# Waiting for the last stores in a section of their own: a grouped convolution on one core

## The chip, the cores and the metric

One core of a Trainium2 chip. The metric is the device time of one execution in microseconds. The program is built once and executed several times, and a difference below 2% counts as "same". An execution has two lengths: the timed number, and the span, which runs from the first to the last instruction recorded by the profile and is 1.8 to 1.9 us shorter in most executions of the kernel before.

## The reference

A 3x3 convolution with padding 1 in 8 groups: 16 images, 64 channels in, 128 out, 64 x 64 pixels, all float32. Cut to its core:

```python
for g in range(groups):
    for b in range(batch):
        for co in range(c_out_per_group):
            for ci in range(c_in_per_group):
                for kh in range(k):
                    for kw in range(k):
                        output[b, g * c_out_per_group + co] += \
                            weight[g * c_out_per_group + co, ci, kh, kw] * \
                            x_pad[b, g * c_in_per_group + ci, kh:kh+h, kw:kw+w]
```

The output is 33.55 MB and the input 16.8 MB.

## The kernel before

GpSimd loads bf16 pieces of the images, VectorE makes two shifted copies of each, TensorE multiplies into eight PSUM banks, ScalarE copies them out to one of five buffers `ob`, and the sync engine stores each buffer with one 2 MB transfer (the first image in two of 1 MB). A store has landed when it has raised its semaphore, a counter that an engine can wait for, by 16 (the trace of before has 272 landings for the 17 stores). The kernel places all waits itself, inside one section that the scheduler leaves alone (`tile_critical`). Cut to the part concerned:

```python
    with tc.tile_critical():
        program(nc, x, weight, out, U, ob, w_sb, wb, mask4, mask, ident, wt, banks)

def program(...):
    ...
    stored = [nc.alloc_semaphore(f"st{i}") for i in range(NOB)]      # NOB = 5
    uses = [0] * NOB
    for b in range(B):                                               # B = 16 images
        slot = b % NOB
        ...                                                          # matmuls, copies to ob[slot]
            if c1 > c0:
                SP.wait(wrote)
                nc.sync.dma_start(outf[b, :, c0:c1], ob[slot][:, c0:c1]).then_inc(stored[slot], 16)
                uses[slot] += 1
        ...
    POOL.wait(SP.done(nc.sync.nop()))
    nc.clear_and_free_semaphores(sems)          # two range clears on GpSimd

    for k in range(B, B + NOB):
        s, val = stored[k % NOB], 16 * uses[k % NOB]
        ...   # the sync engine waits for s >= val, then subtracts val
```

Behind a section the scheduler puts closing code of its own. The sync engine, which holds the section's last work, signals that it is over. All five engines drain (here: each runs one short instruction, with a record of 7 to 46 ns, which waits for that signal and reports that the engine has come so far). The sync engine collects the drains, and then come two barriers, at which every engine waits for all others, with a clear of semaphores between them (in the trace of before GpSimd sees the first one full at 123.124 us, starts the clear at 123.370 and sees the second one full at 123.544). The argument is about this code.

## Time and profile before

| | kernel before |
|---|---|
| timed, median of 3 | 125.62 us (125.61 to 125.66) |
| span of the profiled execution | 123.728 us |
| last instruction of a compute engine ends | 102.84 us |
| last of the five waits starts | 122.603 us |
| from there to the end of the span ("the tail") | 1.125 us |

### The profile page before, as it was taken

What the parts mean: (1) busy time and instruction counts of PE and PEld (TensorE: products, weight loads), DVE (VectorE), ACT (ScalarE), POOL (GpSimd) and SP (SyncE); (2) the same over time, 40 slices, a digit from 0 to 9 for tenths busy, and PEclk for the clock granted to TensorE, in tenths of its full rate; (3) what the DMA queues carried; (4) which work ended last, traced back from release to release, by engine and by line L of the source; (5) the groups of instructions that cost most, each with busy time, mean ns of one, the idle gap of its engine ahead of it and who ended that gap; (6) DMA issues with size and microseconds to landing.
All of it is one profiled execution on the core that took longest, in us unless ns stands there. A gap on an engine that the chain in (4) does not pass through costs nothing.

```text
span 123.7 us, 1308 instructions
## 1 busy us (share of the span) xinstructions
PE 93.3 (75%) x791; PEld 19.1 (15%) x197; DVE 82.3 (66%) x87; ACT 69.4 (56%) x72; POOL 27.8 (22%) x41
## 2 busy tenths in 40 slices
PE   5868999999669999999999999589999970000000
PEld 0011222222112222222222222011111100000000
DVE  3089999999999999999999999999900000000000
ACT  4099867676713776778767493579686782000000
POOL 5997040412230256272450000000000000000000
PEclk9999999999967999999999999999999997555555
DMA  3999999999999999999999999999999999999991
GB/s 75 270 210 217 212 212 297 297 297 331 336 344 339 339 429 363 334 344 350 347 342 339 315 342 368 421 429 424 429 424 434 429 440 445 434 424 424 429 424 69
DMA packets 4374, 42.46 MB, mean 343 GB/s; under 512 B 976, under 2 KB 976, under 8 KB 1360
## 3 DMA queue, kind: packets, MB, share of 16 engines
q1 hardware_dynamic: 2736, 34.38, 66.2%
q0 software_dynamic: 1632, 8.00, 31.5%
q8 instruction: 4, 0.07, 0.2%
q14 instruction: 2, 0.02, 0.0%
HBM read 16.81 MB, written 33.55 MB: 407 GB/s over the span
## 4 chain that ended last, share of the span: by engine, by line
PE 30%; DMA 24%; DVE 20%; ACT 5%; issue 4%; POOLq 0%; SPq 0%
PE banks L256 30%; DMA out_dram<-ob 20%; DVE U L198 20%; ACT ob L272 5%; DMA U<-in_x_dram 4%; DVE wt L214 0%; POOLq L336 0%; SPq L55 0%
## 5 line engine op out<-in xcount | busy, mean ns | idle before, releaser
L256 PE MATMUL banks<-U,wt 96*64 96x504 bf16 (+1 forms) x768 | 87.0, 385 | 5.1 <-DVE U L198 3.2
L198 DVE COPY U<-U 32x4096 bf16<-32x4096 bf16 (+2 forms) x80 | 80.3, 1004 | 5.5 <-DMA U<-in_x_dram 3.0
L272 ACT COPY ob<-banks 128x1024 f32<-128x1024 f32 x64 | 61.4, 1018 | 28.4 <-PE banks L256 19.2
L114 POOL DMA_DIRECT2D U<-in_x_dram x34 | 27.0, 802 | 36.9 <-PE banks L256 35.9
L246 PEld LDWEIGHTS <-wt 96*64 96x64 bf16 x192 | 18.7, 112 | 74.1 <-issue 65.6
L174 PE MATMUL banks<-ob 128*128 128x512 bf16 x20 | 6.1, 469 | 1.5 <-DVE mask L129 1.5
L205 ACT CAST U<-ob 32x1536 bf16<-32x1536 f32 x4 | 5.9, 1469 | 0.1
L165 ACT CAST wb<-w_sb 128x96 bf16<-128x96 f32 x3 | 0.9, 355 | 3.9 <-DMA w_sb<-in_weight_dram 3.9
L165 ACT ACT_TABLE_LOAD x1 | 1.3, 1283 | 1.0 <-SPq L55 1.0
L186 PE MATMUL banks<-ident,wb 128*96 128x128 bf16 x3 | 0.4, 232 | 1.4 <-ACT wb L165 1.4
L186 PEld LDWEIGHTS banks<-ident,wb 128*96 128x96 bf16 x3 | 0.2, 122 | 5.5 <-ACT wb L165 5.5
L128 DVE MEMSET ob<- 128x256 f32 x1 | 0.3, 272 | 1.1 <-SPq L55 1.1
L159 DVE TENSOR_REDUCE mask<-mask 128x4 f32<-128x16 f32 x1 | 0.2, 180 | 0.8 <-POOL mask L147 0.8
L214 DVE TENSOR_TENSOR wt<-banks,mask 96x384 bf16<-96x384 f32 x1 | 0.6, 554 | 0.0
L132 DVE MEMSET U<- 32x448 uint32 x1 | 0.4, 432 | 0.1
L131 DVE MEMSET U<- 32x448 uint32 x1 | 0.4, 432 | 0.0
L172 PEld LDWEIGHTS <-ob 128*128 128x128 bf16 x2 | 0.2, 102 | 1.5 <-DVE mask L129 1.5
L142 POOL TENSOR_SCALAR_AFFINE_SELECT ident<-ident 128x128 bf16<-128x128 bf16 x1 | 0.3, 300 | 0.0
L137 POOL TENSOR_SCALAR_AFFINE_SELECT mask<-mask 128x16 f32<-128x16 f32 x1 | 0.2, 228 | 0.1
L147 POOL TENSOR_SCALAR_AFFINE_SELECT mask<-mask 128x16 f32<-128x16 f32 x1 | 0.2, 214 | 0.0
L322 POOL MEMSET const-float32-0.0<- 128x1 f32 x1 | 0.1, 99 | 0.3 <-issue 0.3
L130 DVE MEMSET ident<- 128x64 uint32 x1 | 0.1, 112 | 0.0
(4 smaller groups left out, 0.4 us busy)
## 6 DMA issues: line engine op xcount, KB each, us to landing
out_dram<-ob SPq DMA_DIRECT2D x15, 2048.0 KB, 20.6
U<-in_x_dram POOLq DMA_DIRECT2D x26, 256.0 KB, 10.3
out_dram<-ob SPq DMA_DIRECT2D x2, 1024.0 KB, 12.7
ob<-in_x_dram SPq DMA_DIRECT2D x1, 768.0 KB, 4.8
U<-in_x_dram POOLq DMA_DIRECT2D x4, 160.0 KB, 5.3
U<-in_x_dram POOLq DMA_DIRECT2D x2, 132.0 KB, 5.0
U<-in_x_dram POOLq DMA_DIRECT2D x2, 124.0 KB, 4.5
w_sb<-in_weight_dram SPq DMA_DIRECT2D x1, 36.0 KB, 4.7
```

Of the source, the lines that this page charges most:

```text
L114: nc.gpsimd.dma_start(place(n, n % 3, h0, h1), xr[32 * n : 32 * n + 32, h0 * W : h1 * W]).then_inc(s, 16)
L131: DVE.done(nc.vector.memset(U[0:32, :, 1, :], 0.0))
L132: zeros = DVE.done(nc.vector.memset(U[64:96, :, H, :], 0.0))
L165: e = ACT.done(nc.scalar.copy(wb[:, kw, :].rearrange("p (j g c) -> p j g c", j=3, g=4), wv[:, kw].unsqueeze(2).to_broadcast([128, 3, 4, CIg]),
L174: nc.tensor.add_instruction(mybir.InstMatmult(name=nc.get_next_instruction_name(), engine=mybir.EngineType.PE, start_tensor_calc=True, sto ...
L186: ins = nc.tensor.matmul(banks[0:96, 0, 128 * kw : 128 * kw + 128], wb[:, kw, :], ident, start=True, stop=True,)
L198: c = DVE.done(nc.vector.tensor_copy(place(n, j, h0, h1), place(n, n % 3, h0, h1)))
L205: need = ACT.done(nc.scalar.copy(place(n, n % 3, 0, RROWS), raw[p0 : p0 + 32, 0 : RROWS * W]))
L214: w_need = DVE.done(nc.vector.tensor_mul(wt[0:96].rearrange("p t (h g c) -> p (t h) g c", h=2, g=4), banks[0:96, 0, 0 : 3 * 128].rearrange ...
L246: pe.ldweights(w_ap, **pos)
L256: ins = pe.add_instruction(mybir.InstMatmult(name=nc.get_next_instruction_name(), engine=mybir.EngineType.PE, start_tensor_calc=kw == 1, s ...
L272: wrote = free[pair] = ACT.done(nc.scalar.copy(ob[slot][:, o0 : o0 + 1024], banks[:, 2 * pair : 2 * pair + 2, :].rearrange("p k n -> p (k ...
```

## The change

Intent: the five waits need the sync engine alone. If they stand in a second section, the first one can be closed while the last stores are still on their way, so the other four engines' drains and the sync engine's waits for them lie under the stores.

```diff
     with tc.tile_critical():
-        program(nc, x, weight, out, U, ob, w_sb, wb, mask4, mask, ident, wt, banks)
+        rest = program(nc, x, weight, out, U, ob, w_sb, wb, mask4, mask, ident, wt, banks)
+
+    with tc.tile_critical():
+        for s, val in rest:
+            count_back(nc, s, val)
+
+def count_back(nc, s, val):
+    num = dict(sync_type="semaphore", id=s.num, ant_name=s.name)
+    nc.sync.add_instruction(mybir.InstEventSemaphore(...))   # wait s >= val, subtract val: as before
@@ end of program()
-    for k in range(B, B + NOB):
-        ...                                                   # the same five instructions
+    return [(stored[k % NOB], 16 * uses[k % NOB]) for k in range(B, B + NOB)]
```

More of the change, by code (lines that the diff above doesn't have):

```diff
@@ L55 @@
     with tc.tile_critical():
-        program(nc, x, weight, out, U, ob, w_sb, wb, mask4, mask, ident, wt, banks)
+        rest = program(nc, x, weight, out, U, ob, w_sb, wb, mask4, mask, ident, wt, banks)
[4 more added lines that the diff above has]
+    num = dict(sync_type="semaphore", id=s.num, ant_name=s.name)
+    nc.sync.add_instruction(mybir.InstEventSemaphore(
+        name=nc.get_next_instruction_name(), engine=mybir.EngineType.SP,
+        sync_info=mybir.SyncInfo(
+            on_wait=[mybir.SyncWait(wait_mode="sem-ge-imm", wait_value=val, **num)],
+            on_update=[mybir.SyncUpdate(update_mode="sem-sub-imm", update_value=val, **num)],
+        ),
+    ))
 class Order:
@@ L294, in program @@
     nc.clear_and_free_semaphores(sems)
-    for k in range(B, B + NOB):
-        s, val = stored[k % NOB], 16 * uses[k % NOB]
-        num = dict(sync_type="semaphore", id=s.num, ant_name=s.name)
-        nc.sync.add_instruction(mybir.InstEventSemaphore(
-            name=nc.get_next_instruction_name(), engine=mybir.EngineType.SP,
-            sync_info=mybir.SyncInfo(
-                on_wait=[mybir.SyncWait(wait_mode="sem-ge-imm", wait_value=val, **num)],
-                on_update=[mybir.SyncUpdate(update_mode="sem-sub-imm", update_value=val, **num)],
-            ),
-        ))
+    return [(stored[k % NOB], 16 * uses[k % NOB]) for k in range(B, B + NOB)]
 _INS = ['x', 'weight', 'groups']
```

## The prediction

> **What bounds the kernel now.** The change can only act after the last store has been issued, so I read the profile from its end: first the slices of the page, then what the sync engine's queue waited for, then a table of stretches of the tail, then the lines of the closing code, and last the starts of single records in the trace.
>
> The page's slices, for the matmuls, VectorE, ScalarE and the DMA engines (each slice is 123.7/40 = 3.1 us):
>
> ```profile
> PE   5868999999669999999999999589999970000000
> ...
> DVE  3089999999999999999999999999900000000000
> ACT  4099867676713776778767493579686782000000
> ...
> DMA  3999999999999999999999999999999999999991
> ```
>
> The compute engines are empty for the last seven slices, some 21 us, while the DMA engines are full up to the last slice. So the end is set by the stores still queued when computing stops. The page's chain of work that ended last stops at the last ScalarE copy (102.84 us), because it follows working instructions; its "DMA out_dram 20%" is an earlier wait for a free buffer, and the last 21 us are not in it. The waits of the sync engine's own queue show them:
>
> ```profile
> engine line waited for: us in total, times, longest us
> SPq L284 <- ACT ob L272: 95.4, 17, 13.1
> SPq L299 <- SPq L299: 19.3, 4, 4.9
> ```
>
> L299 are the five waits that the change moves. They are put down to each other, but what really ended each is a landing of a store. The stretches from the last issue to the end, cut at the five waits:
>
> ```profile
> core 0: us, PE busy (x) PEld busy (x) DVE busy (x) ACT busy (x) POOL busy (x), PEclk, DMA share, GB/s
> 103.00:108.00 5.00, 0.00 (x0) 0.00 (x0) 0.00 (x0) 0.00 (x0) 0.00 (x0) 0.55 0.99 423
> 108.00:112.90 4.90, 0.00 (x0) 0.00 (x0) 0.00 (x0) 0.00 (x0) 0.00 (x0) 0.50 1.00 428
> 112.90:117.70 4.80, 0.00 (x0) 0.00 (x0) 0.00 (x0) 0.00 (x0) 0.00 (x0) 0.50 1.02 437
> 117.70:122.60 4.90, 0.00 (x0) 0.00 (x0) 0.00 (x0) 0.00 (x0) 0.00 (x0) 0.50 0.72 308
> 122.60:123.75 1.15, 0.00 (x0) 0.00 (x0) 0.00 (x0) 0.00 (x0) 0.00 (x0) 0.50 0.00 0
> ```
>
> Four 2 MB stores leave at 423 to 437 GB/s with the DMA share at 1.0: nothing that an engine does in these stretches can make them shorter. Only the last row, 1.15 us without any transfer, is time of instructions. That is all that this change can touch. Two answers on the source lines say what stands there: the five waits, and the scheduler's own closing code on the line where the first section begins.
>
> ```profile
> L299 SPq EVENT_SEMAPHORE  x5: 17/17/17, 103.3 to 122.6; - x5
> ...
> L55 SPq EVENT_SEMAPHORE  x3: 17/28/28, 122.7 to 122.9; - x3
> ...
> L55 ACTq DRAIN  x1: 8/8/8, 122.7 to 122.7; - x1
> L55 POOLq DRAIN  x1: 46/46/46, 122.7 to 122.7; - x1
> ```
>
> The first of the five waits is satisfied at 103.3; the last begins at 122.6. Only after it, at 122.7, does every engine drain. Those five drains wait for nothing but the sync engine's signal, which it gives behind its five waits.
>
> The trace's single records give the tail in nanoseconds. The last data packet of the store queue ends at 122.198 and the last of the 16 landings is recorded at 122.586. The sync engine then starts, in turn: last wait 122.603; signal that the section is over 122.662; drain 122.734; a wait for VectorE's and TensorE's drains 122.808; a wait for its own and ScalarE's 122.882; a no-operation waiting for GpSimd's 122.954; a drain 123.028; a drain that reports to the first closing barrier 123.091. GpSimd sees that barrier full at 123.124; its range clear and a second barrier take until 123.728, the end of the span. In sum 122.603 to 123.091 is 0.488 us on the sync engine, then 0.033 to GpSimd, then 0.604: together 1.125 us.
>
> [...] a wait that held the queue for 4.8 us is a record of 17 ns, and records of 7 to 28 ns start 59 to 74 ns apart. So I cost a step by the distance between starts, never by its recorded length. [...] The trace has 0.39 us from last packet (122.198) to last landing (122.586)[...]. [...] at the start of this trace the sync engine's one is recorded at 33 ns and the next instruction starts 153 ns after its start. [...]
>
> **The change part by part.** No load, copy, matmul, ScalarE copy or store is moved: the comparison of the two built programs differs in line numbers, except on the sync engine, where some rows are new, and in branches at the end.
>
> Moved forward: the signal "section over", the five drains, and the sync engine's waits for the other four. They now come right behind the last issue. The sync engine signals at about 103.3; GpSimd is the last to answer, since its two semaphore clears end at 103.861. The drains then all end by about 104.0. These 0.15 to 0.2 us of the other engines were beside the sync engine's own chain anyway, and now lie under the stores.
>
> Added: an entry into the second section, in the built program one no-operation, three waits and one branch with a wait, all on the sync engine. At 74 ns a step, and 153 ns for the branch, 4 x 0.074 + 0.153 = 0.45 us, from 104.0 to about 104.5. The first wait comes due at 104.5 in place of 103.317, but its store has landed, and the second store lands only at 108.087. So 3.6 us of slack swallow it, and it costs nothing.
>
> Left behind the last wait: signal, drain, a no-operation waiting for that drain, a drain, the drain that reports to the barrier. Seven steps before become five. By the distances of before: 122.603 + 0.059 (signal) + 0.072 (drain) + 0.074 (no-operation) + 0.063 to 0.074 (drain; it waits for nothing now) + 0.063 (report) = 122.934 to 122.945, in place of 123.091. What goes is the two waits for the other engines' drains, 0.146 us, or 0.157 with the lighter drain. The 0.033 and 0.604 behind it stay: both barriers and the clear stand in the end block in both programs, and the other engines already wait there.
>
> Sum: 125.62 - 0.15 = **125.47 us**, 0.12% less. The 1.9 us between the timed 125.62 and the span of 123.7 I leave as they are.
>
> **The rivals.** First, that the whole closing time hides under the stores, which is what one may hope of such a change: 1.125 us off, 124.5 us, 0.9% less. For it: the other four engines are idle for 20 us. Against: the barriers and the final clear follow the second section in the built program, and need the sync engine, which cannot arrive before the last landing.
>
> Second, that nothing is gained: 125.62. For it: the sync engine itself needs the same signal and drain after the last landing, and the slowest other engine might have set the pace. Against: TensorE, the last of the others, reports to the barrier at 122.911, 0.18 us ahead of the sync engine's 123.091. So the sync engine's own chain sets it, and that chain loses two steps.
>
> Third, that it gets slower: the second section adds steps at its exit as well[...]. Exit steps that I take to be free (a branch that falls through) could cost 0.15 us as the measured one did, which just cancels the gain: 125.6. [...]
>
> Fourth, that the stores themselves land at another time. They run one behind the other from about 54 us with full DMA engines, and what comes before is not changed, so only chance moves them. The three runs of before lie within 0.05 us, but another build and another sitting can differ by more than that; I allow some 0.2 us.
>
> **Range and chances.** The step count gives 0.15 us with an uncertainty of one step either way, and chance between builds is larger than that. My range of 8 in 10 is 125.20 to 125.70, a little wider downward, since the first rival ends there in part. For 2%, 2.5 us would have to move. The only stretch the change touches is 1.125 us, so faster by over 2% is impossible by this reading (0.005); slower [...] (0.01); within 2% the rest (0.985).
>
> **What would show it.** In the profile after: the other four engines' drains near 103.3 to 104 instead of 122.7; the last of the five waits still at about 122.6; five sync records from it to the report instead of seven, and 0.97 to 0.98 us from it to the end of the span instead of 1.125. The stretches of the stores should read the same 423 to 437 GB/s. It is wrong if the last wait begins more than 0.2 us away from 122.6 (then the stores moved), if the tail stays at 1.12 us or grows (then the exit of the section costs what I take as free), or if the time falls by much more than 0.2 us (then something in the 1.9 us outside the span depends on the sections).

0.074 us a step and 0.153 us for the branch into the section are distances between starts in the trace of before, and the sum came to 125.62 - 0.15 = 125.47 us. The instruction recorded at 33 ns "at the start of this trace" is the sync engine's compare-and-branch, which also carries a wait.

## The result, and the profile after

Median 125.70 us in 4 runs (125.60 to 125.86) against 125.64 us in 4 runs of before: ratio 1.0001, 95% interval 0.9984 to 1.0019. A ratio is the mean time of one kernel's fast runs over that of the other's of the same rounds, so it is not quite the ratio of the medians quoted.

So the first comparison shows no gain. The profile shows one. The sync engine's own waits in the kernel after (engine and line, what it waited for, us in total, times, longest):

```profile
SPq L301 <- ACT ob L289: 95.5, 17, 12.7
SPq L67 <- SPq L67: 18.1, 4, 4.9
...
SPq L55 <- POOLq L55: 0.4, 1, 0.4
```

L67 are the same five waits. The last row is new: 0.4 us in which the sync engine waits for GpSimd's drain, after the last issue and long before the last landing. The records of the closing code of the two sections, L55 for the first and L59 for the second (duration min/median/max in ns, first and last start in us):

```profile
L67 SPq EVENT_SEMAPHORE  x5: 17/17/17, 104.6 to 122.8; - x5
...
L55 SPq EVENT_SEMAPHORE  x3: 17/28/28, 103.5 to 103.7; - x3
...
L55 ACTq DRAIN  x1: 8/8/8, 103.5 to 103.5; - x1
...
L55 POOLq DRAIN  x1: 46/46/46, 104.1 to 104.1; - x1
...
L59 SPq NOP  x2: 13/13/13, 104.2 to 123.0; - x2
L59 SPq EVENT_SEMAPHORE  x1: 17/17/17, 122.8 to 122.8; - x1
L59 SPq DRAIN  x1: 7/7/7, 122.9 to 122.9; - x1
```

The drains that stood at 122.7 now stand at 103.5 to 104.1, and behind the last wait are only a signal, a drain and a no-operation of the section, then the two drains that lead to the barrier. The stretches, cut at the five waits of this kernel (columns as in the prediction's table; the last two are the DMA share and GB/s):

```profile
103.00:108.00 5.00, 0.00 (x0) 0.00 (x0) 0.00 (x0) 0.00 (x0) 0.00 (x0) 0.65 1.00 429
108.00:113.00 5.00, 0.00 (x0) 0.00 (x0) 0.00 (x0) 0.00 (x0) 0.00 (x0) 0.50 0.99 426
113.00:117.90 4.90, 0.00 (x0) 0.00 (x0) 0.00 (x0) 0.00 (x0) 0.00 (x0) 0.50 1.01 435
117.90:122.75 4.85, 0.00 (x0) 0.00 (x0) 0.00 (x0) 0.00 (x0) 0.00 (x0) 0.50 0.69 297
122.75:123.75 1.00, 0.00 (x0) 0.00 (x0) 0.00 (x0) 0.00 (x0) 0.00 (x0) 0.50 0.00 0
```

The first three stretches have the same rate, 426 to 435 GB/s against 423 to 437 before. In both kernels the rate of the last of them falls before its end (308 and 297 GB/s over its stretch), and its sixteen parts land one after the other: from 121.171 to 122.586 us before, from 121.212 to 122.741 after. The last data packet of their queue ends at 122.198 and 122.405 us, 0.388 and 0.336 us ahead of the last landing. Step by step behind the last wait, starts in us from the traces' records:

| step | before | after |
|---|---|---|
| last of the five waits | 122.603 | 122.757 |
| signal that the section is over | 122.662 | 122.823 |
| the sync engine's own drain | 122.734 | 122.895 |
| wait for VectorE's and TensorE's drains | 122.808 | (at 103.626) |
| wait for its own and ScalarE's | 122.882 | (at 103.696) |
| no-operation (before: waits for GpSimd's drain; after: for its own) | 122.954 | 122.968 |
| drain | 123.028 | 123.012 |
| drain that reports to the first barrier | 123.091 | 123.076 |
| GpSimd sees the barrier full | 123.124 | 123.108 |
| end of the span | 123.728 | 123.712 |

From the last wait to the end: 123.728 - 122.603 = 1.125 us before, 123.712 - 122.757 = 0.955 us after. That is 0.170 us less. But the last store landed 0.154 us later in the profile of after, and nearly all of the gain is gone from the span. Two readings are open. In the first, the later landing is chance. In the second, the change causes it: another build, or closing work that disturbs the stores. If the second is right, the change gains nothing.

### The profile page after: what moved, and what is told of

Read it like the earlier page. It is cut to its first block, busy times and chain, and to the rows that moved or that the text cites. A ratio compares the mean times of both kernels' runs of the same rounds, so it can differ in the third digit from the quotient of the medians.

```text
span 123.7 us, 1316 instructions
## 1 busy us (share of the span) xinstructions
PE 94.1 (76%) x791; PEld 18.5 (15%) x197; DVE 82.2 (66%) x87; ACT 69.4 (56%) x72; POOL 27.7 (22%) x41
## 4 chain that ended last, share of the span: by engine, by line
PE 30%; DMA 24%; DVE 20%; ACT 5%; issue 4%; POOLq 0%; SPq 0%
PE banks L273 30%; DMA out_dram<-ob 20%; DVE U L215 20%; ACT ob L289 5%; DMA U<-in_x_dram 4%; DVE wt L231 0%; POOLq L344 0%; SPq L55 0%
## 5 line engine op out<-in xcount | busy, mean ns | idle before, releaser
L263 PEld LDWEIGHTS <-wt 96*64 96x64 bf16 x192 | 18.1, 111 | 75.3 <-issue 66.8
L191 PE MATMUL banks<-ob 128*128 128x512 bf16 x20 | 6.6, 496 | 1.5 <-DVE mask L146 1.5
```

The costliest lines, as they stand in the source:

```text
L191: nc.tensor.add_instruction(mybir.InstMatmult(name=nc.get_next_instruction_name(), engine=mybir.EngineType.PE, start_tensor_calc=True, sto ...
L263: pe.ldweights(w_ap, **pos)
```

## The experiments

Thirteen profiles were compared: the first ones of before and after, and eleven of the experiments below. Each experiment was timed in five rounds, in three sittings of four, four and three kernels; the kernels of one sitting share 11 runs of the kernel before (means 125.941, 125.939 and 125.896 us). All eleven gave correct results.

**1. The changed kernel again (three times) and the kernel before again.** No edit.

> The changed kernel unchanged, to put it against chance. Theory A (the change gains 0.17 us behind the last landing and leaves the stores alone; the later stores of the first profile were chance): tail from the last wait's start to the end of the span 0.95 to 0.96 us again, the last wait anywhere in 122.4 to 122.9, mean time 0.1 to 0.25 us below the kernel before of the same rounds. Theory B (the new build or the closing work moved up makes the stores land later by as much as the tail is shorter): tail 0.955 again, last wait at 122.75 again (0.1 to 0.2 later than in a profile of before), mean time equal to before within 0.05 us.

> The kernel before, unchanged, against itself: what chance alone does. Theory A: tail 1.12 us, the last wait somewhere in 122.4 to 122.9, not always 122.60; ratio 1.000 with an interval of some 0.1 to 0.2%. Theory B: last wait at 122.60 within 0.03 us, so that the 122.757 of the changed kernel stands out.

> The changed kernel once more, for a third independent set of rounds. The tail from the last wait to the end of the span has been 0.955 us in both profiles of it and 1.125 us in both of before, so if the timed number follows the tail: mean 0.17 us (0.13%) below before, ratio 0.9965 to 1.001 given chance; if the first comparison (ratio 1.0001) was right and something outside the span takes the gain back: ratio 0.999 to 1.001, mean above 0.9995.

> The changed kernel a fourth time, to add rounds to the pool. If the gain is the 0.17 us of the tail: ratio near 0.9987 and, pooled over all four comparisons, a mean difference between -0.05 and -0.30 us; the spans, which leave out what follows the program, lower by 0.1 to 0.3 us as well. If there is no gain: pooled difference within 0.05 us of zero.

| profile | last wait | tail | timed mean (runs) | ratio, 95% interval |
|---|---|---|---|---|
| before | 122.603 | 1.125 | | |
| before_again | 122.764 | 1.125 | 126.18 (6) | 1.0020, 0.9991 to 1.0049 |
| after | 122.757 | 0.955 | 125.72 (4) | 1.0001, 0.9984 to 1.0019 |
| after_again | 122.856 | 0.955 | 125.64 (6) | 0.9977, 0.9957 to 0.9996 |
| after_third | 122.997 | 0.955 | 125.69 (6) | 0.9978, 0.9960 to 0.9996 |
| after_fourth | 123.529 | 0.954 | 125.87 (6) | 0.9997, 0.9968 to 1.0026 |

The five waits in the second profile of before, the same program as the first:

```profile
L299 SPq EVENT_SEMAPHORE  x5: 17/17/17, 103.5 to 122.8; - x5
```

The 122.8 is what the first profile of after had, and the program of before had 122.6 before it. So a landing at 122.75 is not a mark of the change: it occurs in both programs. The changed kernel itself ranges over 122.757 to 123.529. Its last profile has the latest landing of all thirteen, so profiles of one program differ by several times the size of the gain:

```profile
L67 SPq EVENT_SEMAPHORE  x5: 17/17/17, 107.3 to 123.5; - x5
```

The records of the landings show what varies most: the slowest of the sixteen. The mean time of the last store's sixteen landings is 121.754 and 121.826 us in the two profiles of before, and 121.867, 121.832, 121.831 and 121.806 in the four of after. In the last profile of after fifteen had landed by 122.697, and the sixteenth came at 123.512. So no common delay of the stores by 0.15 us is seen. What delays single landings was not tested. It goes with something ahead of the change: computing ended at 105.7 to 106.4 us in the three profiles with a last wait behind 122.9 (after_third, after_fourth and outside_pool of experiment 5), at 102.8 to 104.6 in the other ten. In those three the granted TensorE clock fell to half for longer, or once more, between 75 and 87 us, as the pages' clock rows show (before, after_third, after_fourth; tenths of full speed in 40 slices). So it did in the first profile of experiment 4, whose last wait is not late (122.644):

```profile
PEclk9999999999967999999999999999999997555555
...
PEclk9999999999999999999999996579999999965555
...
PEclk9999999999967999999999999985999999655555
```

Over all four comparisons, 22 runs of after have a mean of 125.73 us and 37 of before 125.90 us: a difference of -0.17 us, with a standard error of 0.065 us worked out from the spread of the two sets. The spans of the three later comparisons (18 and 33) give -0.15 us with 0.07. Both agree with the 0.170 us of the tail. Theory A stands for the size; theory B asked for equal times within 0.05 us and does not fit the pool, although the first and the fourth comparison, taken alone, look like it. The timed runs alone are weak evidence. Comparison by comparison the differences are +0.02, -0.30 (forecast: -0.10 to -0.25), -0.25 and -0.03 us: a mean of -0.14 with a standard error of 0.08 from these four, which does not exclude zero. The pooled runs come from different sittings, which the record numbers as chips 8, 11 and 1. And the kernel before, put against itself, came out 0.24 us slower, more than the gain; its six runs are not in the pool (with them the difference is -0.21 us). So the gain is shown by the tail, in all six profiles, and the timed runs do no more than agree. A shift of the last landing by less than some 0.15 us could not be seen in them.

**2. The entry into the second section laid bare.** The last store is also waited for at the end of the first section, so the entry cannot lie under the stores.

```diff
     with tc.tile_critical():
-        for s, val in rest:
-            count_back(nc, s, val)
+        count_back(nc, *rest[-1])
...
+    for s, val in rest[:-1]:
+        count_back(nc, s, val)
+    nc.sync.wait_ge(*rest[-1])
+    return rest
```

> The changed kernel with the last store also waited for at the end of the first section, so that the entry into the second lies behind the last landing instead of under the stores. If the entry costs what its records' distances show (0.477 us from the first closing no-operation to the section's first instruction, plus the 0.351 us chain that before had): tail 0.351 + 0.477 + 0.319 + 0.032 + 0.604 = 1.78 us, time 126.3 us (0.66 us above before). If section entries are cheap or were paid anyway: tail 1.1 to 1.2, time 125.6.

Measured: 126.64 us (6 runs), ratio 1.0056 (1.0038 to 1.0073), 0.70 us above before (forecast: 0.66); tail 1.919 us, counted from the branch that now holds the last wait. The lines of its two sections:

```profile
L55 SPq COMPARE_BRANCH  x1: 33/33/33, 122.8 to 122.8; - x1
...
L59 SPq NOP  x2: 13/13/13, 123.4 to 124.0; - x2
L59 SPq EVENT_SEMAPHORE  x1: 17/17/17, 123.8 to 123.8; - x1
L59 SPq DRAIN  x1: 7/7/7, 123.9 to 123.9; - x1
```

The way from the first section's closing no-operation (123.283) to the second section's first instruction (123.766) took 0.483 us, where 0.477 was expected from the profile of after. The tail is 0.14 us longer than expected, mostly because the builder moved my extra wait onto the branch that closes the section: from that branch to the signal were 0.158 us, where a plain wait had 0.059 to 0.066. So the entry into a second section took 0.48 us of the sync engine in both profiles, and the changed kernel pays it where it costs nothing: from 104.139 to 104.616, while the second wait begins only at 108.184.

**3. Thirty-two more steps behind the last wait.** Does time behind the last landing pass into the timed number at all?

```diff
+    own = nc.alloc_semaphore("own")          # beside `stored`
...
+    for k in range(32):                      # behind the five waits of the kernel before
+        # the sync engine: wait own >= k (none at k = 0), then own += 1; the last one takes 31 off
+        nc.sync.add_instruction(mybir.InstEventSemaphore(...))
```

> The kernel before with 32 more steps of the sync engine behind its last wait, each waiting for the one before it. If steps behind the last landing pass into the timed number one for one: 32 steps at 59 to 77 ns are 1.9 to 2.5 us, span and time longer by the same, 127.6 to 128.3 against 125.7 to 125.9 of before. If part of the tail lies beside something else that ends later: time up by clearly less than the span.

Measured: 128.03 us (mean of 4), ratio 1.0164 (1.0140 to 1.0189), 2.09 us above before; tail 3.243 us, 2.118 us longer than before.

```profile
L311 SPq EVENT_SEMAPHORE  x32: 17/17/17, 122.8 to 124.8; - x32
```

The tail passes into the time one for one (the interval of the ratio is 1.8 to 2.4 us), and a step of the sync engine that waits for its predecessor takes 2.118/32 = 0.066 us. That the 0.170 us of the tail are not lost behind the span either is seen in the runs of after: timed number less span is 1.83 to 1.93 us in 20 of its 22, as in most runs of before.

**4. All closing behind the stores.** This is the prediction's first rival made real. The waits are put behind the end of the scheduler's context, so the barriers and the clear run under the stores as well.

```diff
-    with tc.tile_critical():
-        for s, val in rest:
-            count_back(nc, s, val)
+    return rest
...  (in the launch code)
-        tile_conv_grouped_2d_kernel(tc, *args)
+        rest = tile_conv_grouped_2d_kernel(tc, *args)
+    for s, val in rest:
+        count_back(nc, s, val)
```

> The five waits behind everything, after the closing barriers, so that these and the final clear run under the stores too. If only the sync engine's last wait is needed after the last landing: the span ends some 0.02 us after the last wait's start, time 125.6 - 1.1 = 124.5 us (0.9% less). Rival: the time between span and timed number (1.9 us) needs all engines after the last landing anyway and grows, so the time falls by less than half of that, to 125.1 or more.

> The version with the waits behind the closing barriers once more. It gained 1.74 us where its span shows 1.1. If that surplus is real: 124.0 to 124.3 again, timed number minus span 1.4 us (1.88 in the other kernels). If it was chance: 124.5 to 124.8.

Measured: 124.17 us (5 runs), ratio 0.9862 (0.9842 to 0.9881), and in another sitting 124.29 us (6), ratio 0.9867 (0.9845 to 0.9889). The tail is 0.017 us in both: the last wait is the last instruction of the span. The drains of the first barrier and the waits in the first of these profiles:

```profile
L342 SPq DRAIN  x3: 7/7/7, 105.8 to 106.1; - x3
...
L65 SPq EVENT_SEMAPHORE  x5: 17/17/17, 106.5 to 122.6; - x5
```

The closing ran at 105 to 106.5 us, under the stores. This version beats the kernel before by 1.3 to 1.4%, and the kernel after of the same rounds by 1.1 to 1.2%. The forecast for the first run, 124.5 us, was too high. The tail explains 1.125 - 0.017 = 1.11 us of the 1.77 and 1.65 us gained. About 0.5 us more lies outside the span: timed number less span is 1.37 to 1.45 us in ten of its eleven runs, against 1.83 to 1.92 us in most runs of before. (Six of before's 33 runs have 2.3 to 2.5, and one of these eleven has 2.0. The spans of single runs are given to 0.1 us.)

**5. Where the surplus comes from.** Three variants of version 4: all five engines end after the last landing (the sync engine adds to one more semaphore, for which the other four wait); the five waits on GpSimd; the five waits on TensorE.

```diff
 # outside_all, behind the five waits
+    tell(nc, nc.sync, over, None, "sem-add-imm", 4)
+    for eng in (nc.tensor, nc.vector, nc.scalar, nc.gpsimd):
+        tell(nc, eng, over, 1, "sem-sub-imm", 1)       # wait over >= 1, take 1 off
 # outside_pool (outside_pe: nc.tensor, PE)
-    nc.sync.add_instruction(mybir.InstEventSemaphore(   engine=mybir.EngineType.SP
+    nc.gpsimd.add_instruction(mybir.InstEventSemaphore( engine=mybir.EngineType.Pool
```

> As the one before, but behind its last wait the sync engine adds to one more semaphore for which the other four engines wait, so that all five engines end after the last landing, a hop (0.06 to 0.1 us) later. If the surplus of some 0.5 us comes from the other four engines having ended early, so that what follows the program on them lies under the stores: it is lost here, 124.6 to 124.8, timed number minus span back at 1.85 to 1.9. If it comes from something else (the barriers' place, the sync engine's end): 124.2 to 124.3, difference 1.4 still.

> The waits behind the closing barriers, on GpSimd instead of the sync engine. If all that counts is that four engines have ended early: 124.1 to 124.3 as on the sync engine, timed number minus span 1.4 us. If what follows the program goes through the engines in a fixed order, the number depends on which one is late: 123.9 or 124.5, difference 1.2 or 1.7.

> The same waits on TensorE's queue. Same two theories: 124.1 to 124.3 with a difference of 1.4 us if it does not matter which engine is late; outside that, and on the other side than GpSimd, if there is an order.

| engine that ends last | mean, us (runs) | ratio, 95% interval | timed less span |
|---|---|---|---|
| sync engine alone | 124.17 (5), 124.29 (6) | 0.9862, 0.9867 | 1.37 to 1.45 |
| TensorE alone | 124.56 (6) | 0.9893, 0.9867 to 0.9918 | 1.67 to 1.75 |
| GpSimd alone | 125.31 (6) | 0.9953, 0.9926 to 0.9979 | 2.27 to 2.42 |
| all five, a hop after the sync engine | 125.03 (6) | 0.9926, 0.9909 to 0.9944 | 2.04 to 2.18 |
| all five, from the closing barrier (before) | 125.9 (33) | 1 | 1.83 to 1.92 in most |

The variant with all five fitted my theory, that it is enough for four engines to end early, only in direction: 124.6 to 124.8 us and a remainder (timed less span) of 1.85 to 1.9 were forecast, and both came out higher. GpSimd refuted the theory: there too four engines end early, and the remainder is the longest of all. The rival's numbers missed too: it put TensorE's remainder on the other side of 1.4 us than GpSimd's, and both are above. Its fixed order of the engines, with 1.2 or 1.7 us, was a guess, and no run shows such an order. What the timed number holds behind the last recorded instruction differed with the engine that was late: of the three tried, shortest for the sync engine (1.37 to 1.45 us), longest for GpSimd (2.27 to 2.42). GpSimd's 2.27 to 2.42 is also about what the six odd runs of before have, which may or may not be the same thing. What the remainder consists of is not in the trace and stays open. A simple rule, each engine's end plus a remainder of its own and the largest of these, does not fit: GpSimd's 2.35 behind its end at 123.640 would give 125.99 us for the profiled run of before, which took 125.61.

## Why the prediction was right

The median, 125.70 us, is at the very edge of the stated range, and the 2% class was right. That the number stayed inside is luck: two of the three later medians of the same kernel, 125.75 and 125.79 us, lie outside. By its steps:

- **The stores set the end, and only the tail can move.** Right. The stretches show the same rates, and what was added or taken behind the last landing (experiments 2 to 4) came out of or went into the time. That no engine could shorten the stores was an inference from the DMA share of 1.0 and was not tested. One reading is wrong: the prediction gives all four stores 423 to 437 GB/s and a DMA share of 1.0, but its own table has 308 and 0.72 for the fourth, whose landings are spread over 1.4 us.
- **Drains and waits moved forward, at no cost.** Right: drains at 103.5 to 104.1, as predicted for 103.3 to 104.0.
- **The entry of 0.45 us lies under the stores.** Right: 104.139 to 104.616 in the profile, for a forecast of 104.0 to 104.5; laid bare it costs 0.48 us. From its branch to the next instruction were 0.155 us, about the 0.153 of the branch at the start of the trace of before. The slack was underrated, since only the last landing counts: in the third profile of after the first wait began at 108.036, 0.4 us ahead of the second, and the tail was 0.955 all the same.
- **Seven steps become five, 0.146 to 0.157 us.** Right in kind, slightly too small: 0.170 us. The forecast put 0.063 to 0.074 us between the no-operation and the next drain. It took 0.044, with a drain that waits for nothing.
- **Branches at the exit of the section, taken to be free.** Right here: behind the last wait the trace of after has no branch record of the sync engine (its two start at 0.9 and 104.5 us), and its steps start 0.044 to 0.073 us apart. Three branches with a wait were measured, the sync engine's first in before, the one into the second section in after and the one that closes the first section in experiment 2, with 0.153, 0.155 and 0.158 us to the next start.
- **The time, 125.47 us.** This is 0.23 us under the measured median. The mechanism was sized well. What was mis-sized is the fourth rival, chance in the last landing: the forecast took the last wait of one profile, 122.603, as the starting point. That is the earliest of the thirteen, which lie between 122.603 and 123.529. The forecast's own allowance of 0.2 us was too small for it; by its own test, the last wait in three of the four profiles of after is "more than 0.2 us away", and no run shows that this came from the change: the mean landing stayed within 0.12 us in all six profiles of the two kernels (experiment 1).
- **The first rival, 124.5 us if the whole closing hides.** Rejected rightly for this change, whose barriers still follow the second section. Built on purpose it gives 124.2 to 124.3, so 1.125 us was a little too small a size for it.
- **The 1.9 us outside the span stay.** Right for this change: 1.86 to 1.92 in the four runs of the first comparison. They are not a constant of the kernel, as experiment 5 shows.

## What to carry to other kernels

When a kernel ends on transfers, look for what its instructions still do behind the last landing, and move everything there that does not need the landing to a place ahead of the wait. Moving the wait into a section of its own took out two steps (0.17 us); moving it behind the closing barriers took out all but one (1.7 us, 0.5 of it outside the span), and the engine that waits last made a difference too (124.2 to 124.3 us for the sync engine, 124.6 for TensorE, 125.3 for GpSimd). Read such small gains from the distances between records (the tail repeated to 0.001 us in the six profiles of the two kernels), and use timed runs only in number: here one comparison of 4 runs with 4 hid the gain completely.
